# Down projections of two SwiGLU layers as 2x2 block products with seven multiplications

## The chip, the cores and the metric

The kernel runs on one core of one Trainium2 chip. Its time is the device time in microseconds of one execution. The engines named below are TensorE (PE, with its weight loads as PEld), VectorE (DVE), ScalarE (ACT), GpSimd (POOL) and SyncE (SP), which issues nearly all DMAs; 16 DMA engines move the data between HBM and on-chip SBUF. Matmuls write into PSUM, which has eight banks of 128 x 512 float32.

## The reference, cut to what matters

```python
def swiglu(h, w_gate, w_up, w_down):
    return (jax.nn.silu(h @ w_gate) * (h @ w_up)) @ w_down

h = x                                   # (1, 1024, 1024) float32
for layer in range(2):
    n = rms_norm(h, norm1_g[layer])
    # layer 0: retention heads and RWKV-7 heads; layer 1: sliding-window attention with sinks
    mix = retention_rwkv_mixer(n, ...) if layer % 2 == 0 else swa_sink_mixer(n, ...)
    h = h + mix
    n = rms_norm(h, norm2_g[layer])
    h = h + swiglu(n, w_gate[layer], w_up[layer], w_down[layer])   # D_FF = 2816
return rms_norm(h, final_g)
```

## The kernel before

Everything is kept transposed: features on the 128 partitions, the 1024 positions in two halves (`hf`) of 512 columns. A tile is 128 x 512 float32; h has 8 tiles a half, the inner layer 22 (f-tiles).

*Products.* float32 values are split into two parts, hi and lo, and a product of a 128 x 128 weight block with a tile is three matmuls: hi with hi, hi with lo, lo with hi (`gemm`, L308 to L314). Weights are split when used (`wsplit`): ScalarE casts hi (L297), GpSimd subtracts to get lo (L298). Activations are split by `split` (L318, L320), lo on GpSimd or DVE.

*Gate and up* are already 2x2 block products with seven multiplications, for a pair of f-tiles: rows are the two f-tiles, columns the two halves, the inner dimension two halves of 4 tiles. `form0` makes the splits of half 0 of the normalised activations (X "11", "21"), `form1` (L1041) those of half 1 and of its sums (t1 to t4, "22"). Two of the seven need half 0 alone: the *early* products (`ffn_early`, L1137; `early`, L1177), whose first is kept in u0. The other five are the *late* products (`late`, L1082): for gate and for up in turn, 12 matmuls a product, with DVE adding PSUM results at L1085 and multiplying silu(gate) by up at L1127. `wsums` (L1105 to L1114) makes the weight sums on DVE from the raw weight tiles (`wq`, six of them in rotation). Of the 11 pairs of a layer, 6 (layer 0) or all (layer 1) do the early products before `form1`; the rest do both together (`whole`). Each finished inner tile is stored in DRAM (`hid`).

*Down* (L1186) runs for each half by itself: six groups of four or three f-tiles; a group loads its inner tiles from `hid`, splits them, and for each of 8 output tiles d splits the weights, does a `gemm` of 12 or 9 matmuls into one of three "f" banks, and DVE adds the bank into h (L1214).

*Order.* Engines execute their instructions in order; the scheduler that builds the program may reorder between them, except where `keep` fixes it. `trunk` fixes the stages: mixer 0; layer 0's early products, form1, late pairs; down of half 0; norm; the first three output tiles of down of half 1; attention 0, beside which the rest of that down runs; then output projection, attention 1, layer 1's early products, form1, late pairs; down of half 0, final norm of half 0, down of half 1, final norm of half 1 (`final`, L1347; multiplications at L1353, stores at L1356). An attention block (4 query blocks x 4 head groups a half) is scores, row maximum (L1295), exponentials (L1302), division (L1308), transposes and the product with v.

## Time and profile before

| | us |
|---|---|
| median of 3 runs | 2523.44 (2523.21 to 2526.51) |
| profiled execution | 2534.11 |
| its span, first to last instruction | 2532.3 |
| mean granted TensorE clock | 0.974 |

The profile is of one execution. Rows of groups read: line, engine, operation, output <- inputs, count | busy us, mean ns of one | idle time of the engine before them <- what ended it. Rows by stretch give the stretch, then for each engine its busy us and instructions, the granted clock, the DMA engines' share and GB/s. Rows of the timeline give start, duration, engine, line and operation. TensorE matmuls overlap: each is listed with 0.39 us, though one starts every 0.23 us.

The stages by the rows of the trace: mixer 0 until about 690 us, gate and up of layer 0 until about 1190, down of layer 0 and attention 0 from there to about 1690, attention 1 and the early products of layer 1 to about 1930, late pairs to about 2280, down of layer 1 and the final norm to the end.

### The profile page before, as it was taken

Reading aid. Unit: us, or ns where it says so; the run is one execution under the profiler, and the core shown is the slowest. Engines: PE = TensorE matmul, PEld = TensorE weight load, DVE = VectorE, ACT = ScalarE, POOL = GpSimd, SP = SyncE. Lnnn points to the kernel's source line nnn. Section 1 sums busy time; section 2 is a strip of 40 time slices with the busy share of each in tenths; the row PEclk is TensorE's granted clock in tenths of the full one; section 3 lists DMA queues with packets and bytes.
Section 4 is the critical chain, followed back from the end, with each engine's and each line's share of the span. In section 5 each row is a group of like instructions: output and inputs, shape, how many; then the busy total and the mean of one; then the engine's idle time right before and its main releaser. Section 6 shows DMA issues by size and latency. Waiting matters only on the chain.

```text
span 2532.3 us, 35543 instructions
## 1 busy us (share of the span) xinstructions
PE 2400.3 (95%) x13074; PEld 1876.7 (74%) x13074; DVE 1444.6 (57%) x2272; ACT 1009.8 (40%) x1840; POOL 1152.1 (45%) x968
## 2 busy tenths in 40 slices
...
GB/s 280 181 207 145 152 187 86 153 131 103 122 142 179 156 144 112 92 72 87 129 144 113 84 92 53 98 127 108 82 142 120 158 125 119 132 80 177 150 174 83
DMA packets 160877, 330.37 MB, mean 130 GB/s; under 512 B 40768, under 2 KB 51648, under 8 KB 160704
## 3 DMA queue, kind: packets, MB, share of 16 engines
q1 hardware_dynamic: 157872, 323.65, 39.1%
...
q8 instruction: 104, 1.70, 0.3%
...
## 4 chain that ended last, share of the span: by engine, by line
PE 62%; DVE 5%; ACT 2%; DMA 2%; issue 1%; POOL 1%; SPq 0%; ACTq 0%; DVEq 0%; POOLq 0%
PE ps_f L314 9%; PE ps_f L312 9%; PE ps_f L313 9%; PE ps_m L1078 5%; PE ps_m L1080 5%; PE ps_m L1079 5%; PE ps_f L1078 2%; PE ps_f L1080 2%; PE ps_f L1079 2%; PE ps_r L1078 2%; PE ps_r L1080 2%; PE ps_r L1079 2%; PE ps_c L1078 2%; PE ps_c L1080 2%; PE ps_c L1079 2%
## 5 line engine op out<-in xcount | busy, mean ns | idle before, releaser
L298 POOL TENSOR_TENSOR w<-wr,w 128x512 fp32r<-128x512 f32 (+1 forms) x432 | 568.3, 1321 | 675.7 <-ACT w L297 647.6
L312 PE MATMUL ps_f<-n,w 128*128 128x512 f32 x1152 | 456.1, 397 | 12.8 <-ACT n L318 4.6
L314 PE MATMUL ps_f<-n,w 128*128 128x512 f32 x1152 | 455.4, 396 | 4.5 <-POOL w L298 4.5
L313 PE MATMUL ps_f<-n,w 128*128 128x512 f32 x1152 | 453.3, 394 | 0.0
L297 ACT CAST w<-wr 128x512 fp32r<-128x512 f32 (+1 forms) x432 | 257.2, 603 | 484.3 <-PE ps_f L314 300.5
L298 POOL TENSOR_TENSOR w<-wq,w 128x512 fp32r<-128x512 f32 x196 | 264.4, 1351 | 291.1 <-ACT w L297 269.1
L216 PE MATMUL ps_f<-n,w 128*128 128x512 f32 x1440 | 382.2, 415 | 5.6 <-DMA w<-wsp 2.8
L216 PEld LDWEIGHTS ps_f<-n,w 128*128 128x128 f32 x1440 | 270.6, 194 | 83.2 <-issue 18.2
L312 PEld LDWEIGHTS ps_f<-n,w 128*128 128x128 f32 x1152 | 218.6, 190 | 64.7 <-issue 9.2
L314 PEld LDWEIGHTS ps_f<-n,w 128*128 128x128 f32 x1152 | 218.3, 189 | 57.4 <-POOL w L298 7.7
L313 PEld LDWEIGHTS ps_f<-n,w 128*128 128x128 f32 x1152 | 218.4, 190 | 48.1 <-issue 2.8
L297 ACT CAST w<-wq 128x512 fp32r<-128x512 f32 x196 | 121.3, 621 | 316.5 <-PE ps_m L1080 205.5
L1214 DVE TENSOR_TENSOR h<-h,ps_f 128x512 f32<-128x512 f32 x192 | 130.5, 681 | 178.2 <-PE ps_f L314 178.1
L1078 PE MATMUL ps_m<-cb,w 128*128 128x512 f32 x440 | 172.9, 393 | 0.6 <-DVE nq L1085 0.6
L1079 PE MATMUL ps_m<-cb,w 128*128 128x512 f32 x440 | 172.1, 391 | 0.0
L1080 PE MATMUL ps_m<-cb,w 128*128 128x512 f32 x440 | 171.8, 391 | 0.0
L1078 PE MATMUL ps_f<-n,w 128*128 128x512 f32 x352 | 142.3, 405 | 10.5 <-ACT u L1180 8.8
L1080 PE MATMUL ps_f<-n,w 128*128 128x512 f32 x352 | 140.2, 400 | 8.2 <-POOL w L298 8.2
L1111 DVE TENSOR_TENSOR ws<-wq 128x512 f32<-128x512 f32 x44 | 42.5, 966 | 181.6 <-DMA wq<-in_w_up 129.5
L1079 PE MATMUL ps_f<-n,w 128*128 128x512 f32 x352 | 140.0, 398 | 0.0
L1078 PEld LDWEIGHTS ps_m<-cb,w 128*128 128x128 f32 x440 | 82.6, 188 | 18.9 <-issue 1.0
L1080 PEld LDWEIGHTS ps_m<-cb,w 128*128 128x128 f32 x440 | 82.6, 188 | 18.8
...
## 6 DMA issues: line engine op xcount, KB each, us to landing
wr<-in_w_down SPq DMA_DIRECT2D x64, 512.0 KB, 3.6
wsp<-w SPq DMA_DIRECT2D x60, 512.0 KB, 3.0
w<-wsp SPq DMA_DIRECT2D x60, 512.0 KB, 3.5
wq<-in_w_gate SPq DMA_DIRECT2D x44, 512.0 KB, 3.8
wq<-in_w_up SPq DMA_DIRECT2D x44, 512.0 KB, 3.3
...
wr<-in_w_in SPq DMA_DIRECT2D x29, 512.0 KB, 4.3
```

Source lines behind the costliest of these rows:

```text
L216: i = self.nc.tensor.matmul(out, lhsT, rhs, **kw)
L297: nc.scalar.copy(hi[:, :n], raw[:, c])
L298: nc.gpsimd.tensor_tensor(out=lo[:, :n], in0=raw[:, c], in1=hi.bitcast(F32)[:, :n], op=ALU.subtract)
L312: nc.tensor.matmul(ps, hi, rh, start=k == 0, stop=False)
L313: nc.tensor.matmul(ps, hi, rl, start=False, stop=False)
L314: nc.tensor.matmul(ps, lo, rh, start=False, stop=k == n - 1)
L1078: mm(ps, hi, xh, start=first and k == 0, stop=False, skip_group_check=True)
L1079: mm(ps, hi, xl, start=False, stop=False, skip_group_check=True)
L1080: mm(ps, lo, xh, start=False, stop=last and k == 3, skip_group_check=True)
L1111: V.tensor_tensor(out=s1, in0=a21, in1=a22, op=ALU.add)
L1214: nc.vector.tensor_tensor(out=hk, in0=hk, in1=ps, op=ALU.add)
```

## The change

Down becomes a 2x2 block product with seven multiplications: rows are two output tiles (2dp and 2dp + 1, four such dp), the inner dimension pairs of f-tiles (`DGROUPS`: groups of four pairs, the last in layer 1 of three), columns the two halves. Both halves are done at once; eight accumulators fill the eight PSUM banks. In layer 0 the last six f-tiles stay plain products (`rest_d`), half 0 at the end of down, half 1 around attention 0.

- *Weight sums* of down are made by DVE in `down` (four operations for each dp of a group); splits go through six rotating buffers (`wtile`: four "w" and two "wr"), in the late pairs too, where `next_w` has five splits issued ahead of the product that uses them.
- *Sums of inner activations* are made by `form_down` beside the late products of the next pair: four DVE subtractions and four splits (hi on ScalarE, lo on GpSimd), stored already split in DRAM (`hc`, 4 x 512 KB a pair) and loaded by `sums8`. The pair before the last in layer 1 stores its sums, and the last pair makes them, inside down's first group, ahead of its fifth product (`owed`, `rest`).
- *Early products* come ahead of the late ones for all 11 pairs of both layers; u0 goes through DRAM for every pair, and the five formerly whole pairs of layer 0 load their first weight tiles again for the late products.
- *form1* is now a generator of four steps that alternate with early pairs; t1 and t2 always use the "n8" tiles.
- *Attention* runs by head groups: two q projections, then the group's four blocks. The norm for attention 1 is issued before the output projection of half 0.
- *Final norm*: ScalarE multiplies h by the gain in place while the squares are made; the last square goes to TensorE by itself; half 0's factor is made before products six and seven of the last group, its multiplications run on GpSimd, half 1's on DVE (five) and GpSimd (three).

```diff
-FGROUPS = [(0, 4), (4, 8), (8, 12), (12, 16), (16, 19), (19, 22)]
-EARLY = (6, 8, 11)
+DGROUPS = [[(0, 4), (4, 8)], [(0, 4), (4, 8), (8, 11)]]
+NP = FT // 2
...
-        for nm in ("22", "t4", "t3", "t1", "t2"):
-            if n8 and nm in ("t1", "t2"):
-                X[nm] = [self.hl(n8, k + 4 * (nm == "t1")) for k in range(4)]
-            else:
-                X[nm] = [[self.t(cb, [P, HT], "cb", 24 if n8 else 40, F32R) for _ in range(2)] for k in range(4)]
+        for nm in ("t1", "t2"):
+            X[nm] = [self.hl(n8, k + 4 * (nm == "t1")) for k in range(4)]
+        for nm in ("22", "t4", "t3"):
+            X[nm] = [[self.t(cb, [P, HT], "cb", 24, F32R) for _ in range(2)] for k in range(4)]
...
+            yield
...
+    def late_splits(self, L, wp):
+        for p in range(NP):
+            raws = [[self.rawtile(wp) for _ in range(2)] for _ in range(2)]
+            for j in range(2):
+                for i, nm in enumerate(("gate", "up")):
+                    self.nc.sync.dma_start(raws[i][j], self.A[f"w_{nm}{L}"][2 * p + j])
+            ws = [self.wsums(r, wp[0]) for r in raws]
+            for nm in ("s2", "s1", "s3", "a22", "s4"):
+                for i in range(2):
+                    yield ws[i](nm)
...
+    def ffn_pair(self, L, p, sp, next_w, form, x):
+        u = self.uses(L, p, sp, x)
+        if p < DGROUPS[L][-1][1]:
+            self.nc.sync.dma_start(x["11"], self.hid[2 * L][2 * p])
+        u0s, gens = [], []
         for i in range(2):
             u0s.append(self.t(sp, [P, HT], "u0", 4))
-            if whole:
-                w = [(lambda r: lambda: self.wsplit(r, HT))(raws[i][0][:, o : o + HT]) for o in (0, HT)]
-                gens.append(self.early(self.pst("f", [P, HT]), w, u0s[i], u[i]))
+            self.nc.sync.dma_start(u0s[i], self.u0d[p, i])
+        for i in range(2):
+            gens.append(self.late(self.pst("m", [P, HT]), self.pst("rc"[i], [P, HT]), next_w, u0s[i], u[i]))
+        self.lockstep(*gens, form)
...
+    def form_down(self, L, p, x, ts):
+        nc = self.nc
+        def put(i, o, a, b):
+            nc.vector.tensor_tensor(out=o, in0=a, in1=b, op=ALU.subtract)
+            t = ts[i - 1]
+            self.split(o, t[:, 0, :], t[:, 1, :])
+            d = (self.hc[L][p, i - 1], t.bitcast(F32))
+            if p == NP - 2:
+                self.owed.append(d)
             else:
-                self.nc.sync.dma_start(u0s[i], self.u0d[p, i])
-        if whole:
-            self.lockstep(*gens)
-        gens = []
-        for i in range(2):
-            gens.append(self.late(
-                self.pst("m", [P, HT]), self.pst("rc"[i], [P, HT]), self.wsums(raws[i], wp[0]), u0s[i], u[i]
-            ))
-        self.lockstep(*gens)
+                nc.sync.dma_start(*d)
+            return o
+        tmp = lambda: self.t(self.pp, [P, HT], "nq", 4)
+        yield
+        t1 = put(1, x["11"], x["12"], x["11"])
+        yield
+        t2 = put(2, tmp(), x["22"], t1)
+        yield
+        put(4, tmp(), x["21"], t2)
+        yield
+        put(3, tmp(), x["22"], x["12"])
+        yield
...
+    def vsplit(self, v):
+        nc, n = self.nc, v.shape[1]
+        w = self.wtile()
+        hi, lo = (w[:, i, : n * P].rearrange("p (k c) -> p k c", c=P) for i in range(2))
+        nc.scalar.copy(hi, v)
+        nc.gpsimd.tensor_tensor(out=lo, in0=v, in1=hi.bitcast(F32), op=ALU.subtract)
+        return [(hi[:, k, :], lo[:, k, :]) for k in range(n)]
...
+    def sums8(self, L, p, i, t):
+        self.keep(self.nc.sync.dma_start(t.bitcast(F32), self.hc[L][p, i - 1]))
+        return t[:, 0, :], t[:, 1, :]
...
+    def down(self, L, fp, fz, rest):
+        op, S = self.vop, self.nc.scalar
+        h0, h1 = (self.kt(self.h[hf]) for hf in range(2))
+        dps = range(KT // 2)
...
+        for g in DGROUPS[L]:
+            n, ps = g[1] - g[0], range(*g)
+            s1, u0 = [], []
+            W = [self.wdown(L, 0, g, fp, "wd0", 5)]
+            X = [plain(0, 2 * p) for p in ps]
+            W += [self.wdown(L, 2 * i, g, fp, "wd0", 5) for i in (1, 2, 3)]
+            for i in dps:
+                W[i] += self.wdown(L, 2 * i + 1, g, fp, "wd1", 6 - L)
+            A = [self.pst(t, [P, HT]) for t in "fffy"]
+            for dp in dps:
+                a11, a12, a21, a22 = W[dp]
+                self.prod(A[dp], self.vsplit(a11), X, True, False)
+                u0.append(self.t(fz, [P, HT], "u0", 4))
+                S.copy(u0[dp], A[dp])
+                s1.append(op(self.wsum(fp, n, 4, 8), a21, a22))
+                op(a21, a11, a21, ALU.subtract)
+                W[dp][0] = op(self.wsum(fp, n, 4, 8), s1[dp], a11, ALU.subtract)
+            X = [self.sums8(L, p, 2, place()) for p in ps]
+            B = [self.pst(t, [P, HT]) for t in "mmrc"]
+            for dp in dps:
+                self.prod(B[dp], self.vsplit(W[dp][0]), X, True, False)
+                y = op(self.t(fz, [P, HT], "y", 2), B[dp], u0[dp])
+                op(h1(2 * dp), h1(2 * dp), y)
+            X = [plain(0, 2 * p + 1) for p in ps]
+            for dp in dps:
+                self.prod(A[dp], self.vsplit(W[dp][1]), X, False, True)
+                op(h0(2 * dp), h0(2 * dp), A[dp])
+                op(W[dp][0], W[dp][1], W[dp][0], ALU.subtract)
+            X = [self.sums8(L, p, 3, place()) for p in ps]
+            for dp in dps:
+                self.prod(B[dp], self.vsplit(W[dp][2]), X, False, False)
+                y = op(self.t(fz, [P, HT], "y", 2), B[dp], u0[dp])
+                op(h1(2 * dp + 1), h1(2 * dp + 1), y)
+            X = [self.sums8(L, p, 4, place()) for p in ps]
+            while self.owed:
+                self.keep(self.nc.sync.dma_start(*self.owed.pop(0)))
+            for _ in rest:
+                pass
+            for dp in dps:
+                self.prod(B[dp], self.vsplit(W[dp][3]), X, False, True)
+                op(u0[dp], B[dp], u0[dp])
+                op(h0(2 * dp + 1), h0(2 * dp + 1), u0[dp])
+            X = [self.sums8(L, p, 1, place()) for p in ps]
+            X6 = [plain(1, 2 * p + 1) for p in ps]
+            if g[1] == NP:
+                yield
+            A = [self.pst(t, [P, HT]) for t in "fffy"]
+            for dp in dps:
+                self.prod(A[dp], self.vsplit(s1[dp]), X, True, False)
+                op(h1(2 * dp + 1), h1(2 * dp + 1), A[dp])
+            for dp in dps:
+                self.prod(A[dp], self.vsplit(W[dp][0]), X6, False, True)
+                op(h1(2 * dp), h1(2 * dp), A[dp])
...
+    def rest_d(self, hf, X, fp=None, raws=(), stop=0):
+        nc = self.nc
+        n = len(X) * P
+        for d in range(KT):
+            raw = raws[d] if d < len(raws) else self.rest_w(hf, d, fp)
+            w = self.wsplit(raw, n)
+            ps = self.pst("f", [P, HT])
+            self.gemm(ps, w, X)
+            hk = self.kt(self.h[hf])(d)
...
-        qt = []
         q8 = self.s8(ap, "q8", 2)
-        for i in range(8):
-            q = q8[i // 4][:, i % 4, :]
-            proj(i, q, scale=0.125, bias=b8[:, i : i + 1])
-            qt.append(q)
-        for b in range(4):
-            for g in range(4):
+        qt = [q8[i // 4][:, i % 4, :] for i in range(8)]
+        for g in range(4):
+            for i in (2 * g, 2 * g + 1):
+                proj(i, qt[i], scale=0.125, bias=b8[:, i : i + 1])
+            for b in range(4):
...
+    def final_r(self, hf, pool, order):
         nc = self.nc
         h = self.kt(self.h[hf])
-        r = self.rstd(h, self.t(pool, [P, HT], "rs", 2))
-        for k in range(KT):
-            n = self.t(self.pp, [P, HT], "nq", 4)
-            nc.vector.scalar_tensor_tensor(
-                out=n, in0=h(k), scalar=self.col("nf", k), in1=r, op0=ALU.mult, op1=ALU.mult
-            )
-            nc.sync.dma_start(self.out[k, :, hf * HT : (hf + 1) * HT], n)
+        ps = self.pst("m", [P, HT])
+        acc = None
+        for i, k in enumerate(order):
+            sq = self.t(self.pp, [P, HT], "nq", 4)
+            nc.scalar.activation(sq, h(k), AF.Square)
+            nc.scalar.activation(h(k), h(k), AF.Copy, scale=self.col("nf", k))
+            if i == 0:
+                acc = sq
+            elif i < KT - 1:
+                nc.vector.tensor_tensor(out=sq, in0=acc, in1=sq, op=ALU.add)
+                acc = sq
+            if i == KT - 2:
+                nc.tensor.matmul(ps, self.cst["ones"], acc, start=True, stop=False)
+        nc.tensor.matmul(ps, self.cst["ones"], sq, start=False, stop=True)
+        r = self.t(pool, [P, HT], "y", 2)
+        nc.scalar.activation(r, ps, AF.Ln, bias=self.cst["eps"][:, 0:1])
+        nc.scalar.activation(r, r, AF.Exp, scale=-0.5)
+        return r
...
+    def final_out(self, hf, r, order, engines):
+        nc = self.nc
+        h = self.kt(self.h[hf])
+        for k, e in zip(order, engines):
+            (nc.gpsimd if e == "p" else nc.vector).tensor_tensor(out=h(k), in0=h(k), in1=r, op=ALU.mult)
+            nc.sync.dma_start(self.out[k, :, hf * HT : (hf + 1) * HT], h(k))
...
+            K.w6 = True
+            ws, q = K.late_splits(L, (wa, wb)), deque()
+            xs, ts = K.stage(stage)
+            nf = DGROUPS[L][-1][1]
+            def next_w():
+                while len(q) < 5:
+                    w = next(ws, None)
+                    if w is None:
+                        break
+                    q.append(w)
+                return q.popleft()
+            for p in range(NP):
+                f = K.form_down(L, p - 1, xs[(p - 1) % 2], ts) if 0 < p <= nf else iter(range(5))
+                K.ffn_pair(L, p, sp, next_w, f, xs[p % 2])
...
+        early(0, sp, 0, 3)
+        early(0, sp, 3, NP, K.form1("n2a", r, K.n8(nb), cb, ft))
...
+        run(K.down(0, fp, fz, ()))
+        K.w6 = False
+        X = [K.rest_x(0, fp, fz)]
+        raws = [K.rest_w(0, d, fp) for d in range(4)]
+        X.append(K.rest_x(1))
+        run(K.rest_d(0, X[0], fp, raws))
...
+        f = K.rest_d(1, X[1], stop=2)
         next(f)
         c0 = K.attn(0, n0, ap, K.n8(nB))
         run(f)
...
+        early(1, sp, 0, 6)
         K.w_o(1, c1)
-        for p in range(EARLY[1], EARLY[2]):
-            K.ffn_early(1, p, sp)
+        r = K.factor_of(1, sp)
+        early(1, sp, 6, 7)
         close(ga)
-        ffn(1, "n2b", sp, EARLY[2], K.n8(K.pp), K.factor_of(1, sp))
-        close(gs, g1)
-        gf, fp = K.pool("ff", "left")
-        run(K.down(1, 0, fp))
-        K.final(0, fp)
-        run(K.down(1, 1, fp))
-        K.final(1, fp)
-        close(gp, gf, K.ghx, gy)
+        gc, cb = K.pool("cb", "right")
+        gt, ft = K.pool("ft", "left")
+        f = K.form1("n2b", r, K.n8(K.pp), cb, ft)
+        next(f)
+        early(1, sp, 7, NP, f)
+        close(gt)
+        x, ts = ffn_late(1, sp, nB)
+        close(gs, gc)
+        gz, fz = K.pool("fz", "left")
+        gf, fp = K.pool("fa", "left")
+        K.w6 = True
+        f = K.down(1, fp, fz, K.form_down(1, NP - 1, x, ts))
+        next(f)
+        order = (0, 2, 4, 6, 1, 3, 5, 7), (1, 3, 5, 7, 0, 2, 4, 6)
+        r0 = K.final_r(0, fz, order[0])
+        run(f)
+        r1 = K.final_r(1, fz, order[1])
+        K.final_out(0, r0, order[0], "pppppppp")
+        K.final_out(1, r1, order[1], "vpvvpvvv")
```

160 lines of the change are left out of this document (90 added, 70 removed).

## The prediction

> **What bounds the kernel now.** I read the page first (span, busy time, chain, groups), then busy time by stretch, then TensorE's waits.
>
> ```profile
> span 2532.3 us, 35543 instructions
> ...
> PE 2400.3 (95%) x13074; PEld 1876.7 (74%) x13074; DVE 1444.6 (57%) x2272; ACT 1009.8 (40%) x1840; POOL 1152.1 (45%) x968
> ...
> PE 62%; DVE 5%; ACT 2%; DMA 2%; issue 1%; POOL 1%; SPq 0%; ACTq 0%; DVEq 0%; POOLq 0%
> ...
> L1214 DVE TENSOR_TENSOR h<-h,ps_f 128x512 f32<-128x512 f32 x192 | 130.5, 681 | 178.2 <-PE ps_f L314 178.1
> ```
>
> TensorE is busy 95% of the span and leads the chain; no other engine reaches 60%. The last row gives the size of what is changed: 192 down products, each ended by one addition into h.
>
> ```profile
> core 0: us, PE busy (x) PEld busy (x) DVE busy (x) ACT busy (x) POOL busy (x), PEclk, DMA share, GB/s
> 0.00:60.00 60.00, 52.42 (x201) 37.87 (x202) 22.15 (x28) 31.60 (x50) 38.18 (x53) 1.00 0.79 279
> 790.00:860.00 70.00, 60.33 (x242) 46.88 (x241) 51.59 (x44) 35.26 (x60) 55.79 (x33) 0.95 0.55 187
> 1195.00:1345.00 150.00, 150.00 (x662) 123.89 (x661) 66.43 (x89) 57.57 (x98) 79.26 (x64) 1.00 0.45 138
> 1455.00:1580.00 125.00, 120.71 (x589) 83.71 (x586) 99.55 (x200) 56.36 (x170) 47.06 (x37) 0.97 0.24 72
> 1930.00:1980.00 50.00, 40.62 (x162) 30.17 (x161) 41.83 (x34) 27.92 (x47) 38.41 (x25) 0.97 0.41 142
> 1980.00:2280.00 300.00, 300.00 (x1314) 246.44 (x1313) 190.49 (x229) 89.76 (x147) 154.16 (x113) 1.00 0.37 121
> 2340.00:2400.00 60.00, 60.00 (x266) 49.67 (x265) 34.33 (x46) 27.63 (x49) 30.19 (x26) 1.00 0.49 150
> 2420.00:2510.00 90.00, 90.00 (x399) 74.55 (x398) 38.22 (x53) 29.25 (x51) 42.43 (x37) 1.00 0.40 122
> 2510.00:2533.00 23.00, 8.47 (x35) 6.05 (x33) 11.35 (x17) 7.04 (x9) 0.89 (x1) 0.76 0.24 91
> ```
>
> The down stages (1195 to 1345 in layer 0; 2340 to 2400 and 2420 to 2510 in layer 1) and the gate/up products (1980 to 2280) have TensorE busy without a gap at a granted clock of 1.00. So there a matmul removed is worth its pitch: 90/399 = 0.2256 us. Idle TensorE stands elsewhere: 9.7 us in 790 to 860 and 9.4 us in 1930 to 1980, where form1 makes the sums of normalised activations, 4.3 us in attention 0 (1455 to 1580), 14.5 us in the tail.
>
> **Matmuls removed.** Before: 2 layers x 2 halves x 8 output tiles x 22 x 3 = 2112 matmuls. After: layer 1 has 7 products x 4 pairs of output tiles x 11 x 3 = 924; layer 0 has 7 x 4 x 8 x 3 = 672, and 2 x 8 x 6 x 3 = 288 for the six f-tiles left plain. That is 1884, or 228 fewer: **-51.4 us** at 0.2256. Nothing hides this gain where TensorE stays full; the other terms ask where it no longer does. The Trainium skill ("TensorE: Matmul & The Clock Gate", section "Back-to-back issue gap") gives some 216 ns for an isolated 512-column matmul, and 131 ns sustained for pairs of load and matmul; by these the term would be -49.2 or -29.9. The 225.6 ns measured here agree with the first and not with the second, and I use the row.
>
> **Form1 spread out.** All eleven pairs now do their first product early in both layers, and form1's four steps alternate with early pairs (from the fourth on in layer 0; around pairs 7 to 10 in layer 1) instead of standing in one block. Its instructions stay. What held TensorE there:
>
> ```profile
> PE ps_f L1078 <- ACT u L1180: 8.8, 7, 1.9
> PE ps_f L1080 <- POOL w L298: 8.2, 6, 3.7
> ```
>
> Both are form1's splits getting ahead of the early products' PSUM copies and weight splits on in-order engines. More TensorE work beside each step thins these waits, but the mechanism stays. Of 9.7 + 9.4 = 19.1 us I take half: **-9.5 us** (bounds 0 and -19.1).
>
> **Tail.** After the last matmul:
>
> ```profile
> 2516.95 0.39 PE L314 MATMUL ps_f<-n,w 128*128 128x512 f32 x1
> 2517.38 0.69 DVE L1214 TENSOR_TENSOR h<-h,ps_f 128x512 f32<-128x512 f32 x1 [1.25 <-PE ps_f L314]
> ...
> 2519.57 1.13 PE L335 MATMUL ps_y<-nq,c_ones 128*128 128x512 f32 x2 [2.23 <-DVE nq L333]
> ...
> 2523.40 2.74 DVE L1353 SCALAR_TENSOR_TENSOR nq<-h,pv,rs 128x512 f32<-128x512 f32 x4 [3.88 <-ACT rs L337]
> ...
> 2526.36 2.75 DVE L1353 SCALAR_TENSOR_TENSOR nq<-h,pv,rs 128x512 f32<-128x512 f32 x4 [0.22 <-DMA out<-nq]
> ```
>
> Eight multiplications (5.5 us) follow the factor. Now DVE has five of them and GpSimd three, the gain is folded in before, and one addition leaves the chain of squares. But half 0's eight GpSimd multiplications and stores come just ahead, GpSimd takes about 1.3 us for an operation, and the activation-table load stays: **-2.5 us** (bounds 0 and -5).
>
> **First group of down in each layer.** Its loads come at once:
>
> ```profile
> q1 hardware_dynamic: 157872, 323.65, 39.1%
> ...
> wr<-in_w_down SPq DMA_DIRECT2D x64, 512.0 KB, 3.6
> ...
> wq<-in_w_gate SPq DMA_DIRECT2D x44, 512.0 KB, 3.8
> ```
>
> 323.65 MB take 39.1% of 2532 us, so the queue moves 327 GB/s while full (the first 60 us: 279 GB/s at a share of 0.79). A group of four pairs needs eight weight tiles (4 MB) and 1 MB of activations before the second product, then 2 MB for each set of pre-split sums. 5 MB take 15 us; the first product lasts 48 x 0.2256 = 10.8 us. Buffers set how early SP may issue: in layer 0 the first inner tiles go into those of t1 and t2, free 72 matmuls (16 us) before the stage. Loads behind the waiting one in SP's order wait too, but nothing of the last late pair. I take +3 for each layer: **+6 us** (bounds 0, if the lead suffices, and 20, if half of 5 MB + 2 MB is uncovered in each).
>
> **Attention 0.** Its filler was layer 0's down of half 1; now it is six f-tiles (8 x 18 matmuls, the first two of the eight ahead of it).
>
> ```profile
> L1214 DVE TENSOR_TENSOR h<-h,ps_f 128x512 f32<-128x512 f32 x24 | 16.1, 673 | 2.5 <-PE ps_f L314 2.5
> L1295 DVE TENSOR_REDUCE st<-s 128x4 f32<-128x1024 f32 x12 | 14.5, 1208 | 0.0
> ```
>
> In 1455 to 1580 there are 12 blocks beside 24 filler chunks (288 matmuls, 65 us). So a block costs DVE (99.55 - 16.1)/12 = 7.0 us and TensorE (120.7 - 65)/12 = 4.6 us. Sixteen blocks are 112 us of DVE against 74 us of their own on TensorE, 43 us of q projections (8 x 24 matmuls, now spread two at a time through the groups) and 24 us of filler: 141 us, enough if spread well. If the last four blocks find none left, 4 x 2.4 = 9.6 us are lost: **+5 us** (bounds 0 and 10).
>
> **Late pairs with sums beside them** (18: eight in layer 0, ten in layer 1; the nineteenth stands in down). This is the least sure term.
>
> ```profile
> L1085 DVE TENSOR_TENSOR nq<-ps_m,u 128x512 f32<-128x512 f32 x44 | 29.9, 682 | 14.1 <-PE ps_m L1080 13.2 <-POOL w L298 0.9
> L1113 DVE TENSOR_TENSOR wq<-ws,wq 128x512 f32<-128x512 f32 x20 | 23.8, 1190 | 0.3
> L1127 DVE TENSOR_TENSOR nq<-nq,nq 128x512 f32<-128x512 f32 x22 | 23.6, 1072 | 1.2
> L1111 DVE TENSOR_TENSOR ws<-wq 128x512 f32<-128x512 f32 x20 | 21.9, 1093 | 64.6 <-DMA wq<-in_w_up 57.9 <-DMA wq<-in_w_gate 5.0 <-POOL w L298 1.2
> ...
> L298 POOL TENSOR_TENSOR w<-wq,w 128x512 fp32r<-128x512 f32 x86 | 114.0, 1326 | 138.1 <-ACT w L297 123.3 <-DVE nq L1085 13.1 <-DMA wq<-in_w_up 1.7
> ```
>
> ```profile
> L1113 DVE TENSOR_TENSOR wq<-ws,wq x44: 672/1500/1780, 803.7 to 2242.6; 128x512 f32<-128x512 f32 x44
> ...
> L1085 DVE TENSOR_TENSOR nq<-ps_m,u x88: 674/683/692, 875.6 to 2266.1; 128x512 f32<-128x512 f32 x88
> ```
>
> The two source rows show minimum, median and maximum. A DVE operation with one input in PSUM (L1085) always takes 0.68 us; one with both in SBUF (L1113) takes 0.67 alone and up to 1.78. Form1's stretch shows what stretches it:
>
> ```profile
> 1951.41 1.75 POOL L320 TENSOR_TENSOR cb<-nq,cb 128x512 fp32r<-128x512 f32 x1
> ...
> 1951.48 0.32 SPq L1147 DMA_DIRECT2D u<-u  x1
> ...
> 1952.03 1.67 DVE L1059 TENSOR_TENSOR ft<-ft,ft 128x512 f32<-128x512 f32 x1
> ...
> 1953.12 1.73 POOL L298 TENSOR_TENSOR w<-wr,w 128x512 fp32r<-128x512 f32 x1
> ```
>
> GpSimd and DVE take turns: one of each in about 1.70 us. A late pair is 120 matmuls, 27.4 us (300/1314 each). Before, DVE has 11 SBUF operations and 10 from PSUM in it (17.4 us of 27.4), GpSimd 10 splits (14.1 us). Each form adds four DVE subtractions and four splits: 15 + 10 on DVE, 14 on GpSimd. DVE's busy time is then 10.2 + 6.8 = 17.0 us if no operation is stretched, 31.3 if 14 are. Today 17.4 - 11 x 0.68 - 6.8 = 3.1 us, about three of 11, are stretched; with GpSimd's share grown from 0.51 to some 0.75 that becomes six of 15, or 23 us. If stretching went by GpSimd's share alone (15 x 0.78 operations) it would be 29.0 us. I stand near the first: the pair keeps its length on average. But in-order DVE has places with little slack: between the third product of gate and the fourth lies one product of up (2.7 us), in which two additions must have read PSUM. A late subtraction ahead of them is then paid by TensorE. I take 0.5 us a pair: **+9 us** (bounds 0 and 3.9 x 18 = 70). SP issues 14 transfers a pair instead of 9; at 0.32 us each that is 4.5 of 27.4 us. Its transfers (2 MB of weights, 2 MB of sums out, 1.5 MB of other tiles: 5.5 MB a pair, 200 GB/s) stay under 327. Loads behind a store that waits for its split lie two products ahead of their use. The Trainium skill says that a DVE operation with both inputs in SBUF contends with a GpSimd operation that reads SBUF, and that the loser blocks for the whole instruction ("SBUF — State Buffer", sections "Who interferes with whom" and "SBUF: two separate sides"). The rows of 0.67 to 1.78 agree in kind; by that rule alone, with a split under way at each subtraction, DVE would need the 31.3 us, the first rival below.
>
> **Inside down.** A group of four pairs is 336 matmuls, 76 us. DVE has 28 SBUF and 24 PSUM operations (35 to 64 us), GpSimd some 34 splits (45 to 58), and 15 MB move (197 GB/s). All fit; where products change sets, an accumulator's read or a load can come late. Five groups at 0.5: **+2.5 us** (bounds 0 and 10).
>
> **Sum.** -51.4 - 9.5 - 2.5 + 6 + 5 + 9 + 2.5 = -40.9 us. The profiled execution took 2534.1 us (span 2532.3 and 1.8 around it), 10.7 above the median of the runs; it would become 2493. The same difference from the median 2523.4 gives **2482.5 us**.
>
> **Rivals.** *DVE bound in the late pairs.* If its wait on a weight load (64.6 us idle ahead of L1111 in eleven pairs) now holds back PSUM reads queued behind it, or contention goes by share, pairs grow. At 29.0 us each (+1.6 x 18 instead of 9): 2502. At 31.3 us each: 2482.5 - 9 + 70 = 2543, slower than before; it turns slower from about 3 us a pair (49.9 + 5 over 18). For it: 1.70 us an alternating pair. Against it: PSUM reads are never stretched, GpSimd has idle time to yield, six buffers of splits run 13 us ahead. *Late transfers.* Both first groups at their upper bound: +14, so 2496. For it: 5 MB against a product of 10.8 us. Against: 16 us of lead. *No losses.* All form1 idle gone, tail -5, the positive terms nought: -51.4 - 19.1 - 5 = -75.5, so 2448. Against it: every seam of before costs something. *The matmuls don't go.* Excluded: the built kernel's order holds 228 fewer of them in down (and two more in the final norm).
>
> **How the numbers follow.** A measurement of this kernel tells 0.2% (5 us) from no change. Forecast 0.62 (2465 to 2495); pairs at about 29 us 0.10; pairs past 3 us of loss 0.08; late transfers 0.10; no losses 0.10. The first, second, fourth and fifth are faster: 0.89 when a little is kept for mixtures near nothing; same 0.03; slower 0.08. The range 2450 to 2512 leaves out the slow rival and part of the lossless one.
>
> **What would show it.** About 226 fewer matmuls of 512 columns; the down stages with TensorE full at 0.2256 us; late pairs of 27.4 to 28 us with DVE at 85% or so and GpSimd at 75%, and TensorE waits on L1085's successors of 0.5 us a pair; form1's stretches with half the idle time; some 3 us idle at the first product of down; up to 5 us in the last blocks of attention 0; 12 to 13 us after the last matmul. I am wrong if late pairs pass 30 us, if down's stretches show TensorE under 97%, or if an unlisted place (the seam between down and attention, the added early products) costs over 10 us.

## The result, and the profile after

| | before | after |
|---|---|---|
| median of 4 runs, us | 2523.32 (2522.62 to 2526.51) | 2550.79 (2546.91 to 2553.05) |
| ratio after/before | | 1.0105, 95% interval 1.0087 to 1.0122 |
| profiled execution, us (span) | 2534.1 (2532.3) | 2546.9 (2545.1) |

The change makes the kernel slower by 27.5 us; the forecast was 2482.5. The page of the kernel after (span, busy time, chain, one group) reads:

```profile
span 2545.1 us, 35353 instructions
...
PE 2365.3 (93%) x12850; PEld 1842.4 (72%) x12850; DVE 1565.7 (62%) x2383; ACT 1034.5 (41%) x1907; POOL 1318.9 (52%) x1050
...
PE 51%; DVE 17%; POOL 11%; DMA 8%; issue 6%; ACT 5%; SPq 1%; DVEq 0%; ACTq 0%; POOLq 0%
...
L1085 PE MATMUL ps_m<-cb,w 128*128 128x512 f32 x232 | 96.2, 415 | 20.3 <-DVE nq L1092 20.3
```

The matmuls did go (13074 to 12850 records). No engine is full: DVE is at 62%, GpSimd at 52%. Yet the chain that ended last now runs through DVE for 17% (before 5%) and through GpSimd for 11% (before 1%). That points at waits between engines rather than at one engine's load. The last row says where: the late products (L1085 with cb) stood idle 20.3 us behind DVE's PSUM additions (L1092).

The part ahead of the first FFN product, which the change does not touch, took 789.8 us in the profile of before and 782.3 in that of after (780 to 789 in the runs below). So stages are compared from there on. Busy time by stage, first of the kernel before, then of the kernel after; the rows are gate and up of layer 0, the middle (down of layer 0, both attentions, early products of layer 1), late pairs of layer 1, down of layer 1, and the tail after its last matmul:

```profile
core 0: us, PE busy (x) PEld busy (x) DVE busy (x) ACT busy (x) POOL busy (x), PEclk, DMA share, GB/s
789.80:1229.30 439.50, 428.95 (x1852) 348.89 (x1851) 238.30 (x277) 149.78 (x252) 238.28 (x166) 0.99 0.35 116
1229.30:1970.10 740.80, 718.15 (x3294) 547.04 (x3293) 411.39 (x708) 349.74 (x764) 333.80 (x258) 0.99 0.33 109
1970.10:2276.90 306.80, 304.99 (x1334) 249.94 (x1333) 197.71 (x233) 95.54 (x157) 161.84 (x118) 1.00 0.37 123
2276.90:2517.00 240.10, 240.10 (x1059) 198.39 (x1057) 120.87 (x159) 90.81 (x152) 115.28 (x94) 1.00 0.47 147
2517.00:2532.30 15.30, 1.47 (x4) 0.30 (x2) 7.47 (x11) 4.51 (x5) 0.00 (x0) 0.67 0.37 137
```

```profile
782.30:918.60 136.30, 125.30 (x531) 99.70 (x530) 57.89 (x54) 60.53 (x105) 86.22 (x60) 0.99 0.48 171
918.60:1244.20 325.60, 312.35 (x1321) 251.77 (x1320) 204.61 (x250) 100.50 (x173) 198.35 (x138) 0.98 0.48 172
1244.20:1965.10 720.90, 691.56 (x3196) 532.32 (x3197) 439.77 (x733) 347.39 (x765) 346.83 (x255) 0.98 0.35 122
1965.10:2295.90 330.80, 315.35 (x1333) 254.00 (x1331) 222.76 (x265) 106.16 (x184) 219.26 (x151) 0.98 0.50 178
2295.90:2521.50 225.60, 214.63 (x928) 175.21 (x928) 164.09 (x184) 92.81 (x161) 154.40 (x109) 0.98 0.56 199
2521.50:2545.10 23.60, 4.15 (x6) 1.13 (x5) 12.15 (x12) 8.32 (x11) 11.67 (x8) 0.65 0.44 167
```

In the second fence gate and up of layer 0 stand as two rows, early products with form1 and late pairs. Stage by stage, against the prediction's terms sorted into the same stages:

| stage | measured | predicted |
|---|---|---|
| gate and up, layer 0 (439.5 to 461.9) | +22.4 | -0.75 |
| middle (740.8 to 720.9) | -19.9 | -17.4 |
| late pairs, layer 1 (306.8 to 330.8) | +24.0 | +5 |
| down, layer 1 (240.1 to 225.6) | -14.5 | -25.3 |
| tail (15.3 to 23.6) | +8.3 | -2.5 |
| sum | +20.3 | -41 |

The two stages from which matmuls went, the middle and down of layer 1, are 34.4 us shorter (42.7 forecast with all their terms, 51.4 by matmuls alone); the late pairs take more than that back. Their loss has two parts of about the same size. In layer 1, 1333 matmuls at 0.2256 us are 300.7 us; TensorE was busy 315.35 and idle 15.45. So 15.5 us are waits (1.8 before), and 14.6 are matmuls that took longer than 0.2256 each (4.0 before). TensorE's waits in the kernel after, in total, how often, and the longest:

```profile
PE ps_m L1085 <- DVE nq L1092: 28.7, 15, 3.0
PE ps_f L1085 <- ACT u L1226: 11.3, 11, 2.0
...
PE ps_f L1086 <- DVE n L327: 6.9, 1, 6.9
PE ps_m L1516 <- DVE nq L1513: 6.7, 1, 6.7
```

The first row is the 15.45 us of layer 1 and the 13.25 (325.60 - 312.35) of layer 0. One such wait in the timeline of the kernel after (start, length, engine, instruction, idle time before it and its releaser):

```profile
1104.07 3.81 POOL L305 TENSOR_TENSOR w<-wq,w 128x512 fp32r<-128x512 f32 x3
...
1105.40 0.33 SPq L1172 DMA_DIRECT2D wq<-in_w_up  x1
...
1108.80 0.88 DVE L1118 TENSOR_TENSOR ws<-wq 128x512 f32<-128x512 f32 x1 [5.89 <-DMA wq<-in_w_up]
...
1113.51 0.69 DVE L1119 TENSOR_TENSOR wq<-wq,wq 128x512 f32<-128x512 f32 x1 [3.83 <-DMA wq<-in_w_up]
1114.12 0.68 DVE L1092 TENSOR_TENSOR nq<-ps_m,u 128x512 f32<-128x512 f32 x1
...
1114.95 0.47 PE L1085 MATMUL ps_m<-cb,w 128*128 128x512 f32 x1 [2.94 <-DVE nq L1092]
```

Read it upwards. TensorE waits 2.94 us, because its next product writes a PSUM bank that L1092 has yet to read. L1092 needs only that bank, but on DVE it stands behind two sums of the *next* pair's weights (L1118, L1119). These wait 5.89 and 3.83 us for their loads while DVE does nothing. The loads were issued late (L1172 at 1105.40), since the raw tiles that they fill are freed by GpSimd's weight splits (L305), which end at 1107.88. The place is the one that the prediction names, between the third product of gate and the fourth. What stands there is not the added subtraction, but older work that now comes later. In the kernel before, in the pair whose first matmul starts at 2112.31, DVE does this at the same place:

```profile
2126.09 0.69 DVE L1111 TENSOR_TENSOR ws<-wq 128x512 f32<-128x512 f32 x1 [6.28 <-DMA wq<-in_w_up]
2126.70 0.68 DVE L1085 TENSOR_TENSOR nq<-ps_m,u 128x512 f32<-128x512 f32 x1
```

There too a sum that waits for its load stands ahead of the read, but only one, and the read ends 15.1 us into the pair, before TensorE needs the bank.

Back in the kernel after, the clock is halved for a while behind that wait of 2.94 us, in its busy time by stretch:

```profile
1115.00:1119.00 4.00, 4.00 (x11) 3.19 (x12) 3.86 (x6) 1.14 (x2) 1.28 (x1) 0.58 0.02 4
```

At a granted clock of 0.58, 11 matmuls stand where 4.00/0.2256 = 17.7 would. The 6.7 that are missing are 1.5 us, so a wait of 2.94 us costs 4.4.

### The profile page after: what moved, and what is told of

Its sections match the earlier page's. It is cut to its first block, busy times and chain, and to the rows that moved or that the text cites. A ratio compares the mean times of both kernels' runs of the same rounds, so it can differ in the third digit from the quotient of the medians.

```text
span 2545.1 us, 35353 instructions
## 1 busy us (share of the span) xinstructions
PE 2365.3 (93%) x12850; PEld 1842.4 (72%) x12850; DVE 1565.7 (62%) x2383; ACT 1034.5 (41%) x1907; POOL 1318.9 (52%) x1050
## 4 chain that ended last, share of the span: by engine, by line
PE 51%; DVE 17%; POOL 11%; DMA 8%; issue 6%; ACT 5%; SPq 1%; DVEq 0%; ACTq 0%; POOLq 0%
PE ps_f L218 7%; PE ps_m L218 5%; POOL w L305 5%; PE ps_f L319 5%; PE ps_f L320 5%; PE ps_f L321 5%; DMA wq<-in_w_up 3%; PE ps_f L1085 3%; PE ps_f L1087 3%; PE ps_f L1086 3%; PE ps_m L1085 2%; POOL wr L305 2%; PE ps_m L1087 2%; PE ps_m L1086 2%; POOL n L327 2%
## 5 line engine op out<-in xcount | busy, mean ns | idle before, releaser
L305 POOL TENSOR_TENSOR w<-wr,w 128x512 fp32r<-128x512 f32 (+1 forms) x276 | 368.6, 1342 | 490.4 <-ACT w L304 465.6
L218 PE MATMUL ps_f<-n,w 128*128 128x512 f32 x1440 | 381.3, 414 | 4.1 <-DMA w<-wsp 2.5
L218 PEld LDWEIGHTS ps_f<-n,w 128*128 128x128 f32 x1440 | 270.4, 194 | 81.6 <-issue 19.5
L304 ACT CAST w<-wr 128x512 fp32r<-128x512 f32 (+1 forms) x276 | 166.6, 612 | 254.5 <-PE ps_f L321 145.1
L305 POOL TENSOR_TENSOR w<-wq,w 128x512 fp32r<-128x512 f32 x118 | 165.1, 1409 | 99.5 <-DVE nq L1092 50.4
L319 PE MATMUL ps_f<-n,w 128*128 128x512 f32 x496 | 199.3, 406 | 10.4 <-ACT n L325 3.6
L320 PE MATMUL ps_f<-n,w 128*128 128x512 f32 x496 | 198.6, 401 | 0.0
L1085 PE MATMUL ps_f<-n,w 128*128 128x512 f32 x453 | 182.3, 405 | 16.4 <-ACT u L1226 11.3
L321 PE MATMUL ps_f<-n,w 128*128 128x512 f32 x496 | 197.2, 399 | 0.3 <-POOL w L305 0.3
L1086 PE MATMUL ps_f<-n,w 128*128 128x512 f32 x453 | 180.7, 399 | 8.4 <-DVE n L327 6.9
L1087 PE MATMUL ps_f<-n,w 128*128 128x512 f32 x453 | 180.8, 401 | 5.9 <-POOL w L305 5.9
L327 POOL TENSOR_TENSOR n<-nq,n 128x512 fp32r<-128x512 f32 x69 | 111.7, 1631 | 56.3 <-ACT n L325 55.1
L1118 DVE TENSOR_TENSOR ws<-wq 128x512 f32<-128x512 f32 x44 | 56.8, 1291 | 125.5 <-DMA wq<-in_w_up 105.9
L319 PEld LDWEIGHTS ps_f<-n,w 128*128 128x128 f32 x496 | 94.8, 192 | 35.7 <-issue 4.7
L1085 PEld LDWEIGHTS ps_f<-n,w 128*128 128x128 f32 x453 | 86.7, 191 | 45.5 <-ACT u L1226 16.7
L1085 PE MATMUL ps_m<-cb,w 128*128 128x512 f32 x232 | 96.2, 415 | 20.3 <-DVE nq L1092 20.3
L304 ACT CAST w<-wq 128x512 fp32r<-128x512 f32 x118 | 72.3, 617 | 103.6 <-PE ps_m L1087 43.5
L320 PEld LDWEIGHTS ps_f<-n,w 128*128 128x128 f32 x496 | 94.8, 191 | 24.5 <-issue 4.7
L321 PEld LDWEIGHTS ps_f<-n,w 128*128 128x128 f32 x496 | 94.6, 191 | 23.1 <-issue 1.9
L1086 PEld LDWEIGHTS ps_f<-n,w 128*128 128x128 f32 x453 | 86.7, 191 | 28.9 <-DVE n L327 7.3
L1087 PEld LDWEIGHTS ps_f<-n,w 128*128 128x128 f32 x453 | 86.8, 192 | 27.1 <-POOL w L305 7.6
L305 POOL TENSOR_TENSOR wr<-wq,wr 128x512 fp32r<-128x512 f32 x58 | 80.5, 1392 | 44.9 <-DVE nq L1092 23.3
```

The lines of the kernel that those rows point to most:

```text
L218: i = self.nc.tensor.matmul(out, lhsT, rhs, **kw)
L304: nc.scalar.copy(hi[:, :n], raw[:, c])
L305: nc.gpsimd.tensor_tensor(out=lo[:, :n], in0=raw[:, c], in1=hi.bitcast(F32)[:, :n], op=ALU.subtract)
L319: nc.tensor.matmul(ps, hi, rh, start=k == 0, stop=False)
L320: nc.tensor.matmul(ps, hi, rl, start=False, stop=False)
L321: nc.tensor.matmul(ps, lo, rh, start=False, stop=k == n - 1)
```

## The experiments

The kernels are numbered as they were made; there is no e9. The medians of the kernel before lie between 2523 and 2528 us in the different sets, so each kernel stands as a ratio to those of its own set. Lengths of the two late stages and of the other stages come from the profiles, in us. In e5 and e14 the row of layer 1 holds 22 matmuls of early products more than in the others (5 us).

| kernel | median | ratio [95%] | early L0 | late L0 | late L1 | down L1 | tail |
|---|---|---|---|---|---|---|---|
| after | 2550.8 | 1.0105 [1.0087, 1.0122] | 136.3 | 325.6 | 330.8 | 225.6 | 23.6 |
| e1 | 2612.0 | 1.0336 [1.0304, 1.0367] | 140.0 | 351.7 | 357.9 | 224.3 | 23.3 |
| e2 | 2524.5 | 0.9993 [0.9978, 1.0007] | 136.1 | 311.3 | 316.7 | 225.1 | 23.4 |
| e3 | 2552.6 | 1.0106 [1.0076, 1.0135] | 136.1 | 327.1 | 331.4 | 227.3 | 23.5 |
| e4 | 2552.3 | 1.0108 [1.0076, 1.0140] | 136.2 | 327.5 | 331.2 | 227.1 | 22.4 |
| e5 | 2568.4 | 1.0160 [1.0138, 1.0181] | 136.3 | 332.6 | 346.9 | 226.1 | 23.3 |
| e6 | 2523.0 | 0.9985 [0.9973, 0.9998] | 136.2 | 310.0 | 316.7 | 224.5 | 23.3 |
| e7 | 2546.5 | 1.0079 [1.0051, 1.0107] | 127.7 | 326.0 | 331.5 | 226.0 | 21.2 |
| e8 | 2545.9 | 1.0068 [1.0047, 1.0090] | 136.2 | 324.6 | 331.1 | 223.3 | 23.3 |
| e10 | 2561.3 | 1.0134 [1.0111, 1.0157] | 140.0 | 326.4 | 330.3 | 223.7 | 22.9 |
| e11 | 2501.1 | 0.9890 [0.9870, 0.9910] | 128.8 | 310.9 | 316.5 | 215.4 | 19.7 |
| e12 | 2545.7 | 1.0063 [1.0040, 1.0087] | 136.1 | 324.7 | 327.7 | 226.8 | 23.3 |
| e13 | 2558.1 | 1.0122 [1.0106, 1.0138] | 136.1 | 330.2 | 332.6 | 227.0 | 23.3 |
| e14 | 2540.5 | 1.0054 [1.0040, 1.0069] | 129.9 | 332.2 | 342.2 | 217.4 | 18.4 |
| e15 | 2542.6 | 1.0070 [1.0047, 1.0094] | 132.6 | 326.4 | 329.8 | 218.5 | 19.0 |

**e1: is it the order on DVE alone?** The sums of weights are held where the code has them, behind the PSUM reads that the scheduler had put them ahead of.

```diff
-        V.tensor_tensor(out=s1, in0=a21, in1=a22, op=ALU.add)
+        self.keep(V.tensor_tensor(out=s1, in0=a21, in1=a22, op=ALU.add))
```

> One line differs from the changed kernel: the first of the four weight sums of a late pair is pinned on DVE behind everything written ahead of it, so that it can't be issued before the two additions that read PSUM after the third product. All work stays. Theory 1 (order: DVE waits for a weight load with those PSUM reads queued behind it, TensorE waits 1.0 to 3.4 us a pair for them, and the longer waits halve its clock for another 3.4 us): the gaps go, a late pair takes 27.2 to 28 us instead of 29.6 to 33, and the kernel 30 to 48 us less, 2503 to 2520. Rival (load: DVE and GpSimd are too busy with the added sums): the same work takes as long, the gaps only move to other places, 2540 to 2555.

It became 2.3% slower than the kernel after. TensorE's waits of e1:

```profile
PE ps_c L1085 <- ACT wr L304: 27.9, 6, 4.7
PE ps_c L1085 <- ACT w L304: 21.4, 6, 3.6
PE ps_m L1085 <- ACT w L304: 15.4, 7, 3.7
```

The wait on L1092 has left the top of the list. In its place TensorE waits for the casts of the sums (L304), because the sums now come too late for the products that use them. Both orders of DVE lose, so putting the reads first does not help by itself.

**e2 and e3: which of the added parts?** e2 leaves out the subtractions and splits of the sums of inner activations (except in the first and the last pair) and keeps their loads and stores. e3 leaves out the stores of these sums for all pairs but the first and the last two, and reads the first pair's in their place.

```diff
# e2
-            nc.vector.tensor_tensor(out=o, in0=a, in1=b, op=ALU.subtract)
             t = ts[i - 1]
-            self.split(o, t[:, 0, :], t[:, 1, :])
+            if p == NP - 1 or p == 0:
+                nc.vector.tensor_tensor(out=o, in0=a, in1=b, op=ALU.subtract)
+                self.split(o, t[:, 0, :], t[:, 1, :])
# e3
-            else:
+            elif p == NP - 1 or p == 0:
                 nc.sync.dma_start(*d)
```

> Left out: the sums of inner activations beside late pairs (the four DVE subtractions and four splits of each), but for the first and the last pair of a layer; their stores and loads stay, so later results differ. Load rival: without the added DVE and GpSimd work the stalls go entirely, as before the change, 27.5 us a pair, about 2505. Theory 1: the weight sums stay ahead of the PSUM reads; only as far as the added splits delayed the weight loads are the waits shorter: 28 to 29.5 us a pair, 2515 to 2540.

> Left out: the stores of the pre-split sums of nearly all pairs (2 MB a pair); down loads the first pair's sums in their place, so that loads, sums and splits stay and results differ. Third theory (SP and the DMA queue: stores that wait for their splits stand ahead of the weight loads in SP's order): the weight loads come earlier and at least half of the gaps goes, 2515 to 2535. Theory 1 and the load rival: SP's loads wait for the weight splits that free their buffers anyway, so less than 8 us is gained, 2543 to 2553.

Without subtractions and splits the late pairs shrink by 14.3 and 14.1 us; without the stores nothing changes (325.6 to 327.1, 330.8 to 331.4). The added arithmetic costs this, the stores do not.

**e6: the four splits on DVE.** Nothing is left out; the low parts of the added sums are made by DVE in place of GpSimd.

```diff
-            self.split(o, t[:, 0, :], t[:, 1, :])
+            self.split(o, t[:, 0, :], t[:, 1, :], False)
```

> All work stays; the lo parts of the added sums (four splits beside a late pair) are made by DVE instead of GpSimd. Theory 4: the four splits (5 to 7 us) leave GpSimd's part of the loop, DVE's part grows by less, since it stands idle 9 us a pair: pairs of 27.5 to 29 us, 2510 to 2535. Load rival with GpSimd as the engine that is short: the same. Load rival with DVE as the engine that is short (or the shared access): pairs grow past 31 us, above 2560.

The late pairs are as short as in e2 (310.0 and 316.7), and the kernel comes level with the one before. So the four subtractions, and four more operations on the fuller engine, cost nothing that shows. The 28 us hang on where four splits a pair are made, on GpSimd or on DVE. The same place of the loop in e6's timeline, in a pair whose first matmul starts at 1061.2:

```profile
1069.21 0.39 SPq L1172 DMA_DIRECT2D wq<-in_w_up  x1
...
1073.81 1.08 DVE L1118 TENSOR_TENSOR ws<-wq 128x512 f32<-128x512 f32 x1 [4.44 <-DMA wq<-in_w_up]
...
1076.58 1.10 DVE L1119 TENSOR_TENSOR wq<-wq,wq 128x512 f32<-128x512 f32 x1 [1.69 <-DMA wq<-in_w_up]
1077.61 0.68 DVE L1092 TENSOR_TENSOR nq<-ps_m,u 128x512 f32<-128x512 f32 x1
```

The first load is issued 8.0 us into the pair and the second sum ends at 16.5. TensorE reaches the place after 72 matmuls, 16.2 us. In the kernel after, the same two times are 10.0 and 18.8 in the pair shown above, and 8.7 and 16.8 in the one that follows: the waits are long and short by turns. The engines are not full in either kernel, as their busy time by stretch shows, first after, then e6:

```profile
1000.00:1200.00 200.00, 189.22 (x796) 152.37 (x795) 135.62 (x164) 64.33 (x112) 136.92 (x93) 0.97 0.52 187
```

```profile
1000.00:1200.00 200.00, 196.61 (x849) 158.84 (x848) 149.83 (x201) 69.60 (x119) 113.70 (x70) 1.00 0.54 192
```

Both have slack (DVE 68 and 75%, GpSimd 68 and 57%), and the one with the busier DVE is the faster. What these timelines show to be short is time around a loop: GpSimd's split frees a raw tile, SP issues its load, it lands 4 to 5 us later, DVE makes the sums, ScalarE casts them, GpSimd splits them. Added splits in that queue make the loop longer than a pair, though GpSimd has idle time elsewhere.

**e12 and e13: does the price follow the number, or the place?** In e12 the first two of the four sums are split by DVE, in e13 the last two.

```diff
-            self.split(o, t[:, 0, :], t[:, 1, :])
+            self.split(o, t[:, 0, :], t[:, 1, :], i > 2)   # e12
+            self.split(o, t[:, 0, :], t[:, 1, :], i < 3)   # e13
```

> All work stays; only two of the four lo parts of each pair's sums (the first two made) are moved from GpSimd to DVE. Theory 4, a loop that decides only while it is longer than the 27.2 us that TensorE needs: the loop was about 30.5 us with four splits of some 1.5 us in it, with two it is 27.5, so most of the gain is there already: 2524 to 2531. Price theory (each added split on GpSimd costs TensorE the same): half the gain, 2534 to 2540.

> All work stays; the lo parts of the last two sums made in each pair are on DVE, those of the first two stay on GpSimd: the other half of the split that gave 2546. Place theory (these two wait for their subtractions in front of the first weight splits of the next pair, so splits, freed tiles and weight loads all come late): most of the gain, 2522 to 2531. Number theory: as the other half, 2540 to 2548.

Neither theory's range was met. Half of the splits moved brings 4 us of the late stages' 30 in e12; in e13 these stages even grow by 6 us. In e13's timeline a split that stayed on GpSimd (L327) stands right ahead of the three that free raw tiles, and waits for its own cast:

```profile
1108.18 1.30 POOL L327 TENSOR_TENSOR n<-n,n 128x512 fp32r<-128x512 f32 x1 [2.00 <-ACT n L325]
1109.44 3.78 POOL L305 TENSOR_TENSOR w<-wq,w 128x512 fp32r<-128x512 f32 x3
```

The idle 2.00 us are in the loop, and the next loads follow at 1110.75. In e12 GpSimd is idle 1.8 us there for a weight cast. So the price is not a sum over splits; an in-order wait at this place seems to be enough. That reading of e12 and e13 was not tested by itself.

The two runs do speak against two rivals. If GpSimd's load were the limit, less of it would help; from 918 to 1244 us GpSimd is busy 198.75 us in the kernel after, 179.29 in e12 and 172.19 in e13, while layer 0's late pairs take 325.6, 324.7 and 330.2. If it were contention (DVE's sums stretched while GpSimd works, from which the prediction sized its first rival), a run in which the two sums ahead of the read are short would be fast. The first of them in the kernel after, in e6 and in e12:

```profile
L1118 DVE TENSOR_TENSOR ws<-wq 128x512 f32<-128x512 f32 x44 | 56.8, 1291 | 125.5 <-DMA wq<-in_w_up 105.9 <-POOL wr L305 9.3 <-POOL w L305 6.2
L1118 DVE TENSOR_TENSOR ws<-wq 128x512 f32<-128x512 f32 x44 | 40.1, 911 | 94.8 <-DMA wq<-in_w_up 83.0 <-POOL wr L305 7.0 <-DMA wq<-in_w_gate 3.3
L1118 DVE TENSOR_TENSOR ws<-wq 128x512 f32<-128x512 f32 x44 | 41.4, 942 | 97.5 <-DMA wq<-in_w_up 76.0 <-POOL wr L305 11.3 <-POOL w L305 5.8
```

The second (L1119) takes 1128, 859 and 767 ns. So both are about as short in e12 as in e6, and still e12 gains only 4 us of the 30.

**e10: e6 with the order of e1.** Both edits together:

```diff
+        self.keep(V.tensor_tensor(out=s1, in0=a21, in1=a22, op=ALU.add))
...
+            self.split(o, t[:, 0, :], t[:, 1, :], False)
```

> All work stays: the added sums' lo parts on DVE, and the weight sums pinned behind the PSUM reads, the two edits that alone gave 2523 and 2612. If the pin is bad only because the loop of loads, sums and splits was already longer than a pair: with four splits out of the loop it costs little, 2515 to 2530, and the waits of 1.4 to 2.0 us left in layer 1 go. If sums issued late are what starves TensorE in any case: pairs of 30 us or more again, above 2560.

With the splits on DVE and the sums held behind the PSUM reads, the late stages are as long as in the kernel after (326.4, 330.3): the sums are late again for their casts. With e1 this shows that the order of reads before sums does not pay in either kernel.

**e5, e14 and e15: earlier loads.** e5 gives f1's raw tiles two alternating pairs of buffers (f2 has the other two of the six), so that loads can start sooner. e14 is the same edit on e11 (below), e15 adds e1's.

```diff
-            raws = [[self.rawtile(wp) for _ in range(2)] for _ in range(2)]
+            raws = [[self.t(wp[i // 4], [P, 1024], f"wq{i}", 1) for i in (p % 2 * 2 + n, 4 + n)] for n in range(2)]
```

> All work stays; only which of the six raw weight tiles a late load goes into is changed: the first f-tile's weights of gate and up take tiles 0, 1 and 2, 3 in turn by pairs, the second f-tile's always tiles 4, 5. Before, the loads of a pair stood in SP's order behind one that waits for the ninth of the ten splits of the pair ahead; now two are free a pair ahead and the other two wait for the seventh and eighth. Theory 4 (a loop sets the period: load, sums on DVE, splits on GpSimd with the added splits between, and only then the tile for the next load; no engine is full): the loop loses about two splits and a load's place, late pairs go from 29.6 and 33 us (early and late average with the first pairs 29.6 to 30.1) to 27.3 to 28.5 us, the kernel to 2505 to 2530. Load rival (DVE and GpSimd capacity): no change, 2545 to 2555.

> All work stays: the four edits of the 2501 us kernel, and the raw weight tiles assigned as in the run that gave 2568. If what is left in the late pairs (311 and 316.5 us against 298 for the matmuls) is the wait for loads: 305 or less each, 2485 to 2496. If DVE's order is what is left (this assignment makes all eight weight sums stand in front of the PSUM reads): 2505 to 2530.

> All work stays: the four edits of the 2501 us kernel, the raw tiles that let the loads come earlier (alone: 2540), and the weight sums pinned behind the PSUM reads (with DVE splits alone: 2561). If order and loads are the two halves of the late pairs' waits, together they go: pairs of 27.2 to 28 us, the two late stages 298 to 308 us each, 2480 to 2497. If sums behind the reads are too late for the next pair's first splits even with early loads: pairs of 29 us or more, 2515 to 2550.

All are slower than what they start from, and none meets the time that the loop was to give: e5's late pairs take 30 to 31 us where 27.3 to 28.5 were forecast. So the loop is read from timelines, and no run has shortened it without changing the order too. In e14 the loads do come sooner (6 us into a pair), and the scheduler then puts all eight sums ahead of the reads; from its timeline, the first and the last of them and the read:

```profile
1049.12 1.27 DVE L1123 TENSOR_TENSOR ws<-wq 128x512 f32<-128x512 f32 x1 [3.35 <-DMA wq<-in_w_gate]
...
1056.66 0.69 DVE L1126 TENSOR_TENSOR wq<-wq 128x512 f32<-128x512 f32 x1
1057.27 0.68 DVE L1097 TENSOR_TENSOR nq<-ps_m,u 128x512 f32<-128x512 f32 x1
```

So DVE makes eight sums of 0.7 to 1.8 us in a row before it turns to the read, and TensorE waits 2.0 us for that. With the order held in e15 it waits for casts again (17.5 us in 13 waits), and the late stages are as long as in e10 (326.4 and 329.8, against 326.4 and 330.3), so there the time of the loads makes no difference. Earlier loads alone, and earlier loads with a held order, both fail. Which order of all three engines would bring the late pairs to the 27.1 us of their matmuls (120 x 0.2256) is open.

**e4, e8 and e7: the start of down, the tail, form1.** At the start of down in layer 1, DVE in the kernel after does this:

```profile
2298.54 1.65 DVE L1202 TENSOR_TENSOR n<-n,n 128x512 f32<-128x512 f32 x1
...
2303.45 1.74 DVE L1202 TENSOR_TENSOR nq<-n 128x512 f32<-128x512 f32 x1
2305.12 1.28 DVE L327 TENSOR_TENSOR n<-hr,n 128x512 fp32r<-128x512 f32 x2
```

The last pair's four subtractions (L1202), meant for down's fifth product, stand ahead of the two splits (L327) that down's first product needs. TensorE waits 6.9 us for these, the third row of its waits above. e4 holds the subtractions in the code's order. e8 also spreads them, a step at a time between the products of down's second group.

```diff
# e4 and e8
-            nc.vector.tensor_tensor(out=o, in0=a, in1=b, op=ALU.subtract)
+            s = nc.vector.tensor_tensor(out=o, in0=a, in1=b, op=ALU.subtract)
+            if p == NP - 1:
+                self.keep(s)
# e8
+        step = lambda: next(rest, None) if g[0] == 4 else None
...
-            for _ in rest:
-                pass
+            step()
# e7, in form1: casts held in the code's order; for half 1 the final norm of the kernel before
-        nc.scalar.copy(hi, src)
+        i = nc.scalar.copy(hi, src)
+        if self.pin:
+            self.keep(i)
```

> Two pins, all work stays. First: the last pair's four subtractions, written ahead of the fifth product of down in layer 1, are pinned there on DVE instead of ahead of the splits that the second matmul of that stage waits for. Second: the last three additions of the squares of half 1 are issued behind the last addition into h. If order is the cause: the 7.3 us gap and the halved clock after it at the start of down in layer 1 go (10 to 13 us), and the 23.6 us after the last matmul shrink to 18 to 20 (4 to 5 us): 2533 to 2538. If the start waits for its loads and the tail for GpSimd's eight multiplications: under 4 us together.

> All work stays; the four sums of layer 1's last pair, which only down's third group needs, are made one at a time beside the second group's first products and pinned there on DVE, instead of together in the first group. The run before this one moved them to the first group's fifth product, and the gap went with them (6.7 us there for 7.3). If the bunch of four subtractions, splits and stores is what stalls: both gaps go, down of layer 1 takes 212 to 218 us from its first to its last matmul instead of 225.6, the kernel 2537 to 2543. If the first group lacks its loads: 223 us or more, 2547 to 2553.

> Two places, no work left out. Tail: half 1's final norm as before the change (one matmul with ones, multiplication by gain and factor together on DVE), half 0's as changed. If the two small matmuls at a lowered clock (3.9 us against 1.1) and the copies by ScalarE made the tail longer: 23.5 us after the last matmul become 17 to 20. If half 0's factor on ScalarE and its eight GpSimd multiplications did: over 21. Form1: the casts of its splits are pinned on ScalarE in the order written, behind the copies of the early products ahead of them. If casts issued too soon make the early products wait (11 us in 11 waits): the early stage of layer 0 goes from 136 to 124 to 130 us. If DVE and GpSimd are what form1 lacks: no shorter than 134. Together 2535 to 2550.

e4 shortens the wait of 6.9 us at the start to 1.2, but a wait of 6.3 us comes behind the fifth product: the sums are then made at one stroke, and the load for the sixth product stands in SP's order behind their four stores (SP issues these until 2355.95, the load at 2356.05). Its other edit, in the tail, gains 1.1 us of the 4 to 5 forecast, and the kernel as a whole is no faster. In e8 both long waits are gone, two smaller ones (0.9 and 2.5 us) come at 2455 to 2460, and down is 2.3 us shorter, less than the 8 to 14 forecast. e7's held casts shorten layer 0's early part from 136.3 to 127.7 us, so its idle time came from where form1's casts stood among others on ScalarE; in layer 1 the same edit costs a wait of 6.9 us at the first late product. Its tail is 21.2 us, 2.4 shorter; by the terms set for it (over 21) that speaks for half 0's factor and GpSimd's eight multiplications as what still costs there.

**e11: what gained, together.** e6's splits, e8's spreading (in the second group), e7's held casts in layer 0 alone, and a tail with one matmul of ones a half and all 16 multiplications, with the gain, on DVE; half 0's come behind half 1's additions of squares.

```diff
+            self.pin = g == "n2a"
...
+            self.split(o, t[:, 0, :], t[:, 1, :], False)
...
-        r1 = K.final_r(1, fz, order[1])
-        K.final_out(0, r0, order[0], "pppppppp")
-        K.final_out(1, r1, order[1], "vpvvpvvv")
+        r1 = K.final_f(1, fz, order[1])
+        with tc.issue_after(K.ladd.ins):
+            K.final_m(0, r0, fp, "hr")
+        K.final_m(1, r1, K.pp, "nq")
```

> All work stays. Four edits together, each on its own stage: the added sums' lo parts on DVE (late pairs, -28 us in its run), the last pair's sums spread over the second group of down in layer 1 (-2), form1's casts pinned in layer 0 alone (-8.5 there; in layer 1 the pin gave 5 us back), and a new tail: both factors as before the change with one matmul, half 0's multiplications on DVE behind half 1's squares instead of on GpSimd (23.5 us become 17 to 20). If the stages add up: 2505 to 2512, faster than the kernel before by 0.5 to 0.8%. If they feed one another's waits: 2515 to 2525.

It is 1.1% faster than the kernel before (ratio 0.9890, 0.9870 to 0.9910), 2501 us, and by the two ratios 2.1% faster than the kernel after. Busy time by stage of e11, from late pairs of layer 1 to the tail:

```profile
1940.30:2256.90 316.60, 309.29 (x1334) 249.47 (x1333) 233.69 (x305) 108.60 (x184) 172.31 (x110) 1.00 0.52 186
2256.90:2472.20 215.30, 212.48 (x925) 174.57 (x926) 167.54 (x190) 85.66 (x150) 147.88 (x102) 0.99 0.57 208
2472.20:2491.90 19.70, 2.51 (x4) 0.51 (x3) 14.21 (x21) 4.51 (x5) 0.00 (x0) 0.60 0.57 213
```

Down is now 24.8 us shorter than before, close to the predicted 25.3. Late pairs and the tail still give some of it back. The changes to the tail were made at once, so their shares are not known.

## Why the prediction was wrong, step by step

- **Matmuls removed (-51.4): right.** With the losses forecast beside it, the gain is there where no long wait eats it: the middle -19.9 of -17.4, down -24.8 of -25.3, the latter only once e11 had taken its waits away.
- **Late pairs (+9): this step failed.** They lost 22.0 in layer 0 (325.6, against 303.6 of before without the early products that it had among its late pairs) and 24.0 in layer 1, 46 in all or 2.6 us a pair. I had priced engines by their load, and the load itself came out below what I allowed for: 23 us of DVE a pair predicted, 222.76/11 = 20.3 measured. But what set the time was when one PSUM read comes in DVE's order, behind loads, sums and splits that wait for each other, and I counted the four splits added on GpSimd only as load. The first rival names the wait (DVE on a weight load, PSUM reads queued behind it), and it is what happened. Its size, however, was worked out from contention, and the chance of the slower size set at 0.08 because "GpSimd has idle time to yield"; the idle time is real and lay at other places. e6 shows it: 28 us back by moving splits to the busier engine. That the path is the loop from a freed raw tile to the next one is the reading of the timelines.
- **What is left of the 46.** e2 and e6 still have some 17 us over before. e6's waits on L1092 sum to 11.4 us. In e2 the added arithmetic is gone, so these 17 us come from something else in the change. It also issues splits five ahead across pairs and moves more through DRAM; the first was not taken out by itself, and of the second only the stores were (e3), with the arithmetic in place.
- **Halved clock: not in the sum.** A wait was priced at its own length. In layer 1's late pairs slower matmuls cost 10.6 us more than before, beside 13.7 us more of waits. About 6 of the 10.6 are the halved clock: in e11, at a granted clock of 1.00 in this stage, 8.3 of the 14.6 us are still there (309.29 - 1334 x 0.2256).
- **Form1 (-9.5): nothing came.** 17.2 us of layer 0's early part are not matmul time (136.3 - 528 x 0.2256), 16.6 before. Spreading alone did not help; holding the casts did (e7, -8.6).
- **First group of down (+3 in layer 1): wrong cause and size.** I counted loads; the long wait was DVE's order (e4, e8). There were waits of 1.6 and 6.9 us, and after them 4.4 us of matmuls at half clock (2305.85 to 2310.28), which lose half of that: 10.7 us.
- **Tail (-2.5): +8.3 measured.** The half finished early, before the change, had its norm out of the way before the last matmul; now both end together. In the kernel after, GpSimd's eight multiplications run beside DVE's last additions of squares:

```profile
2518.02 11.71 POOL L1527 TENSOR_TENSOR h<-h,y 128x512 f32<-128x512 f32 x8 [6.59 <-ACT y L1520]
...
2524.11 1.60 DVE L1513 TENSOR_TENSOR nq<-nq,nq 128x512 f32<-128x512 f32 x1 [0.69 <-ACT nq L1508]
...
2528.53 0.68 DVE L1264 TENSOR_TENSOR h<-h,ps_y 128x512 f32<-128x512 f32 x1
2528.66 2.08 PE L1516 MATMUL ps_m<-nq,c_ones 128*128 128x512 f32 x2 [6.73 <-DVE nq L1513]
```

  The additions take 1.60 us in place of 0.68. They alternate on DVE with the last additions into h, so the last of these (L1264) starts at 2528.53, 7.0 us after the start of the last matmul of down; before the change it was 0.4 us (2516.95 to 2517.38). The prediction had seen these GpSimd operations "just ahead" and priced only their own time.
- **Attention 0 (+5), inside down (+2.5): no loss that shows.** The middle, which holds attention 0 and layer 0's down, came out 2.5 us better than its terms; they were not measured one by one.
- **Not settled.** The two profiled executions differ by 12.8 us, the medians by 27.5. Of the gap, 7.5 us are the untouched first part; the other 7 us are not in these two traces.
